# Attention blocks taken in six pairs, with TensorE's row halves and column halves in alternation

## The chip, the cores and the metric

The kernel runs on one core of a Trainium2 chip. The metric is the device time of one execution in microseconds (us); lower is better. The engines are named as the profile names them: PE (TensorE, the matrix multiplier; PEld is its weight load), DVE (VectorE), ACT (ScalarE), POOL (GpSimd) and SP (SyncE, which here only issues DMAs). Each engine works through its own list of instructions in order, and semaphores hold an instruction back until what it reads has been written.

## What is computed

A two-layer decoder trunk on 256 tokens of width 1024: a feed-forward block (SwiGLU), a Mamba-2 mixer, a feed-forward block, the shared keys and values, a feed-forward block, sliding-window attention, a feed-forward block. The change touches the attention alone:

```python
def sliding_window_attention(u, k, v, w_q, q_norm, sinks, rel_bias, w_o):
    q = rmsnorm((u @ w_q).reshape(bsz, t, KV_HEADS, GROUP, HEAD_DIM), q_norm)
    ...
    def block(args):
        s = jnp.einsum('bqkrd,bskd->bkrqs', qk, kk) * scale + bias
        s = jnp.where(valid, s, -jnp.inf)
        m = jnp.maximum(jnp.max(s, axis=-1, keepdims=True), sink)
        p = jnp.exp(s - m)
        denom = jnp.sum(p, axis=-1, keepdims=True) + jnp.exp(sink - m)
        return jnp.einsum('bkrqs,bskd->bqkrd', (p / denom), vk)
    o = lax.map(block, (qb, kb, vb, jnp.arange(nb)))
    return o.reshape(bsz, t, HEADS * HEAD_DIM) @ w_o
```

There are 16 heads of 64, two key/value heads (eight query heads share one), and two tiles of 128 tokens; the first tile sees 128 keys, the second 256.

## The kernel before

All products with weights are made in a split form: a weight tile `raw` is loaded by DMA, ACT casts it to a rounded part `wh` (line 167), DVE subtracts to get the rest `wl` (line 168), and PE adds three products (`wh,vh`, `wl,vh`, `wh,vl`). The products inside attention, queries with keys and weights with values, are plain float32, and each of those matrix products is two passes in the trace.

The attention has these steps, by the names in the code. Below, t is the tile of tokens (0 or 1) and g the key/value head (0 or 1).

- Queries of tile t, head group g: 24 products into a bank `pq` (`q_mm`). `q_norm` then takes ACT (square, line 955), DVE (sum, line 957), POOL (power, line 218, output `rq`) and DVE (multiply, line 960, output `qn`). `q_turn`, called Q, transposes `qn` on PE into `ptq`, and ACT copies it to `qT` (line 971).
- The work on heads is cut into 12 blocks. A block of tile 0 has four heads of 128 keys, a block of tile 1 has two heads of 256 keys. Even blocks use the lower 64 partitions of `qT` and `kT` (row half 0 of PE), odd blocks the upper 64.
- `scores` (Sc): PE writes `ps`; DVE copies the sink into the last column of `sp`, and one custom instruction for each head adds the bias and takes the maximum (`CUSTOM_DVE_ANT_0` in the trace, `ISA` in the lists below); DVE negates it to `nmx`.
- `expo` (E): ACT, one exponential for each head, with the sum in `den`.
- `divide` (D): DVE, reciprocal `rd` and one multiplication for each head.
- `weights_T` (W): PE transposes `sp` into `ptp`; ACT copies it to `pT` (line 985).
- `values` (V): PE multiplies `pT` with the values into `po`; even blocks write PSUM partitions 0 to 63 (column half 0), odd ones 64 to 127. After the last block of a (t, g), ACT casts `po` into `uT` and DVE writes the rest of it (both through `act` and `dve`).

`act` and `dve` chain these steps on ACT and DVE in the order of the calls. With `strict` set, PE's instructions stand exactly in the order of the code. Between the blocks stand fills, one for each call of `F(1)`: three products of the queries of g = 1 (16 fills), and then three products of the output projection `pa` for the first half of the heads (32 fills). The splits of `w_o`, which those need, go to ACT and DVE between the other work, from the time when the buffers of `w_q` come free.

Before, the queries of both tiles of g = 0 are computed with the weight tiles in the outer loop, and the statistics of the norm (`cur.stats`, PE's `pc`) come 42 products into them. Then the loop runs over 12 blocks with these lags: W four blocks behind Sc, V five, E one, D two. `ps` has two banks of its own; `ptp` and `po` share two banks (`ps_tr`). `sp` has five buffers.

Of the kernel before, what the change touches and what calls it, by code (L numbers as in the profile page):

```python
# [18 lines left out]
P = 128  # L19
# [21 lines left out]
def yoco_kernel(ctx: ExitStack, tc: tile.TileContext, a: dict, out: bass.AP):  # L41
# [896 lines left out]
    def attention(ap, cur, kT, vtok, bias, nxt):  # L938
# [52 lines left out]
        def scores(n):  # L991
            t, g, b, nh = blocks[n]
            qT = qTs[t, g]
            L = (t + 1) * P
            i = b % 2
            p0 = (b // 2) * nh
            ps = ps_mm.tile([P, nh, L], F32, tag="mm", name=nm("ps"))
            sp = ap.tile([P, nh, L + 1], F32, tag="sp", name=nm("sp"), bufs=5)
            mx = sb.tile([P, 4], F32, tag="mx", name=nm("mx"), bufs=5)
            nmx = sb.tile([P, 4], F32, tag="nmx", name=nm("nmx"), bufs=5)  # L1000
            den = sb.tile([P, 4], F32, tag="den", name=nm("den"), bufs=5)
            rd = sb.tile([P, 4], F32, tag="rd", name=nm("rd"), bufs=5)
            hs = [(p0 + x) * 2 + i for x in range(nh)]
            for x in range(nh):
                j = p0 + x
                mm(ps[:, x, :], qT[i * DH:(i + 1) * DH, j * P:(j + 1) * P],
                   kT[g][i * DH:(i + 1) * DH, 0:L], True, True)
            dve(nc.vector.tensor_copy, sp[:, :, L], snk[:, g * 8 + hs[0]:g * 8 + hs[-1] + 1:2])
            for x in range(nh):
                hh = g * 8 + hs[x]  # L1010
                dve(nc.vector.tensor_tensor_reduce,
                    out=sp[:, x, 0:L], in0=ps[:, x, :], in1=bias[g][:, hs[x], S - L:S],
                    scale=1.0, scalar=snk[:, hh:hh + 1], op0=ALU.add, op1=ALU.max,
                    accum_out=mx[:, x:x + 1])
            dve(nc.vector.tensor_scalar_mul, nmx[:, 0:nh], mx[:, 0:nh], -1.0)
            sps[n] = sp, nmx, rd, den

        def expo(n):
            sp, nmx, rd, den = sps[n]
            for x in range(blocks[n][3]):  # L1020
                act(nc.scalar.activation, sp[:, x, :], sp[:, x, :], AF.Exp,
                    bias=nmx[:, x:x + 1], accum_out=den[:, x:x + 1])

        def divide(n):
            t, g, b, nh = blocks[n]
            L = (t + 1) * P
            sp, nmx, rd, den = sps[n]
            dve(nc.vector.reciprocal, rd[:, 0:nh], den[:, 0:nh])
            for x in range(nh):
                dve(nc.vector.tensor_scalar_mul, sp[:, x, 0:L], sp[:, x, 0:L], rd[:, x:x + 1])  # L1030
# [13 lines left out]
        def values(n):  # L1044
            t, g, b, nh = blocks[n]
            nk = t + 1
            i = b % 2
# [4 lines left out]
            for kk in range(nk):  # L1052
                mm(po[i * DH:(i + 1) * DH, p0 * P:(p0 + nh) * P],
                   vtok[kk][:, g * DH:(g + 1) * DH], pTs[n][:, kk, :], kk == 0, kk == nk - 1)
            if b == 8 // nh - 1:
# [45 lines left out]
        later(42, cur.stats)  # L1101
        strict[0] = True
        pqs = [q_bank() for t in range(NT)]
        for k in range(KT):
            for t in range(NT):
                q_mm(pqs[t], t, 0, k)
        for t in range(NT):
            q_norm(pqs[t], t, 0)
        F(5)
        Q(0, 0)  # L1110
        F(1)
        fills = (2, 2, 2, 2, 1, 1, 0, 0, 0, 0, 0, 5, 5, 5, 5, 4, 4)
# [126 lines left out]
```

## Time and profile before

| | us |
|---|---|
| median of 3 runs | 1044.66 (1044.32 to 1045.03) |
| the profiled execution's own time | 1044.65 |
| its span, first to last instruction | 1042.9 |
| PE, DVE, ACT, POOL busy in the span | 1031.1, 738.8, 605.6, 56.1 |
| attention on PE, from the first `pq` to the first `pm` behind it | 769.9 to 852.3 of the span |

A row of the time line has the start (us from the span's start), the duration, the engine, the line, the operation, the output and inputs by the program's names, the array tile (`64*128` is 64 rows by 128 columns), the shape and the number of merged instructions; in brackets stands how long the engine idled before it and what ended that. Lines 102 and 989 and 985 are helpers, so the steps are told apart by their tiles.

### The profile page before, as it was taken

The page shows a single profiled execution, that of the slowest core. Times are in us where ns is not written, and L with a number is a line of the kernel's source. Part 1 is how long each engine was busy: PE and PEld are TensorE (multiplying, and loading weights), DVE is VectorE, ACT ScalarE, POOL GpSimd, SP SyncE. Part 2 cuts the span into 40 slices and gives each one's busy share as a digit, 9 for nine tenths or more (in the row PEclk, how much of TensorE's full clock was granted, in tenths as well). Part 3 has the DMA queues.
Part 4 walks back from the last instruction along what each step waited for, and adds up shares of the span by engine and source line. Part 5 has one row for each costly group of instructions (what it writes and reads, how often), then busy time and mean ns, then how long its engine had stood idle before and what let it go on. Part 6 is the DMA issues. An engine that isn't in the chain of part 4 may idle for free.

```text
span 1042.9 us, 17921 instructions
## 1 busy us (share of the span) xinstructions
PE 1031.1 (99%) x7096; PEld 942.7 (90%) x7096; DVE 738.8 (71%) x1260; ACT 605.6 (58%) x1048; POOL 56.1 (5%) x78
## 2 busy tenths in 40 slices
PE   9999999999999999999999999999999999999998
PEld 8999999999999999999998999999986699888887
DVE  6965656789999889656556975665677678565654
ACT  7654545668966656454545754454566665454552
POOL 1200000003210010000000000010002000000000
PEclk9999999999999999999999999999999999999999
DMA  8665556557455364746566556584641336464641
GB/s 283 200 219 196 185 180 209 157 176 247 163 160 184 124 204 162 233 160 213 162 203 194 169 164 201 165 294 163 229 162 41 122 106 214 166 209 158 216 145 41
DMA packets 138981, 187.17 MB, mean 179 GB/s; under 512 B 5005, under 2 KB 120881, under 8 KB 138897
## 3 DMA queue, kind: packets, MB, share of 16 engines
q1 hardware_dynamic: 136560, 179.32, 52.6%
q0 software_dynamic: 2288, 6.69, 2.3%
q8 instruction: 55, 0.90, 0.4%
q14 instruction: 30, 0.24, 0.1%
q10 hardware_dynamic: 48, 0.02, 0.0%
HBM read 184.90 MB, written 1.11 MB: 178 GB/s over the span
## 4 chain that ended last, share of the span: by engine, by line
PE 68%; issue 21%; DVE 5%; DMA 2%; POOL 2%; ACT 1%; SPq 0%; POOLq 0%; DVEq 0%; ACTq 0%
PE pm L104 36%; PE acc L104 17%; PE pa L104 5%; PE pp L104 3%; DVE wl L168 2%; PE pq L102 2%; PE pa L102 1%; PE ps L102 1%; PE po L102 1%; DVE sp L989 1%; DMA xin<-in_x_dram 1%; DMA raw<-in_ssm_w_out_dram 1%; PE pkv L104 1%; PE py L104 1%; DMA raw<-in_ssm_w_in_dram 1%
## 5 line engine op out<-in xcount | busy, mean ns | idle before, releaser
L168 DVE TENSOR_TENSOR wl<-raw,wh 128x1024 fp32r<-128x1024 f32 (+1 forms) x372 | 411.7, 1129 | 82.2 <-ACT wh L167 80.5
L167 ACT CAST wh<-raw 128x1024 fp32r<-128x1024 f32 (+1 forms) x372 | 347.1, 970 | 108.7 <-PE acc L104 44.7
L104 PE MATMUL pm<-uT,wh 128*128 128x512 f32 x1152 | 403.1, 392 | 0.8 <-DVE tp L326 0.8
L104 PE MATMUL pm<-uT,wl 128*128 128x256 f32 x1152 | 321.5, 280 | 0.0
L104 PEld LDWEIGHTS pm<-uT,wh 128*128 128x128 f32 x1152 | 216.1, 188 | 46.5 <-ACT wdth L532 1.0
L104 PEld LDWEIGHTS pm<-uT,wl 128*128 128x128 f32 x1152 | 216.6, 188 | 0.9
L104 PE MATMUL acc<-ghl,wh 128*128 128x256 f32 x1056 | 191.5, 282 | 1.6 <-DVE ghl L344 1.4
L335 ACT COPY lo<-pm 128x256 f32<-128x256 f32 x144 | 53.2, 369 | 205.9 <-PE pm L104 205.9
L104 PEld LDWEIGHTS acc<-ghl,wh 128*128 128x128 f32 x1056 | 162.2, 188 | 4.9 <-DVE ghl L344 1.9
L336 DVE TENSOR_TENSOR tp<-pm,lo 128x256 f32<-128x256 f32 x144 | 60.9, 423 | 135.4 <-ACT lo L335 135.3
L104 PE MATMUL acc<-ghl,wl 128*128 128x256 f32 x528 | 148.2, 282 | 0.0
L104 PE MATMUL pp<-uT,wh 128*128 128x256 f32 x576 | 104.9, 283 | 0.1
L104 PEld LDWEIGHTS acc<-ghl,wl 128*128 128x128 f32 x528 | 99.4, 188 | 0.0
L104 PEld LDWEIGHTS pp<-uT,wh 128*128 128x128 f32 x576 | 88.6, 189 | 0.5 <-DVE uT L300 0.3
L104 PE MATMUL pp<-uT,wl 128*128 128x256 f32 x288 | 80.5, 281 | 0.0
L104 PE MATMUL pm<-vh,wh 128*128 128x256 f32 x256 | 73.2, 286 | 0.0
L104 PE MATMUL pm<-vh,wl 128*128 128x256 f32 x256 | 72.5, 283 | 0.0
L104 PE MATMUL pm<-vl,wh 128*128 128x256 f32 x256 | 72.4, 283 | 0.0
L104 PE MATMUL acc<-wh,ghl 128*128 128x512 f32 x176 | 58.3, 395 | 0.0
L343 ACT CAST ghl<-g 128x256 fp32r<-128x256 f32 x88 | 35.4, 403 | 32.9 <-DVE g L340 32.5
L104 PEld LDWEIGHTS pp<-uT,wl 128*128 128x128 f32 x288 | 54.1, 188 | 0.2 <-issue 0.2
L344 DVE TENSOR_TENSOR ghl<-g,ghl 128x256 fp32r<-128x256 f32 x88 | 37.0, 422 | 17.7 <-ACT ghl L343 17.7
(234 smaller groups left out, 1268.1 us busy)
## 6 DMA issues: line engine op xcount, KB each, us to landing
raw<-in_ffn_w_dram SPq DMA_DIRECT2D x168, 512.0 KB, 4.9
raw<-in_ffn_w_dram SPq DMA_DIRECT2D x44, 1024.0 KB, 5.3
raw<-in_ssm_w_in_dram SPq DMA_DIRECT2D x16, 1024.0 KB, 5.4
raw<-in_ssm_w_out_dram SPq DMA_DIRECT2D x8, 1024.0 KB, 5.2
raw<-in_ssm_w_in_dram SPq DMA_DIRECT2D x8, 512.0 KB, 5.1
pr<-pdram POOLq DMA_DIRECT2D x8, 512.0 KB, 4.4
raw<-in_w_q_dram SPq DMA_DIRECT2D x4, 1024.0 KB, 4.9
raw<-in_w_o_dram SPq DMA_DIRECT2D x4, 1024.0 KB, 4.8
```

What stands on the lines that cost most here:

```text
L102: r = op(*args, **kw)
L104: r = op(*args, **kw)
L167: return (nc.scalar.copy(wh, rs).ins, nc.vector.tensor_sub(wl, rs, wh.bitcast(F32)).ins)
L168: nc.vector.tensor_sub(wl, rs, wh.bitcast(F32)).ins)
L335: nc.scalar.copy(lo, pw[:, 256:512])
L336: nc.vector.tensor_add(o, pw[:, 0:256], lo)
L343: nc.scalar.copy(gh, g)
L344: nc.vector.tensor_sub(gl, g, gh.bitcast(F32))
L989: chain[1] = op(*args, **kw).ins
```

## The change

The loop runs over six pairs of blocks instead of 12 blocks. In a pair, Sc alternates its products between the two row halves and two `ps` banks; V alternates between the two column halves of `po`. The copy of the sink goes from DVE to POOL (`nc.gpsimd`), `sp` and its companions get six buffers. The queries of tile 0, g = 0 are computed in full before those of tile 1, and the statistics come 20 products in. The order within one round m is W of the first block of pair m-2, Sc of pair m, E of pair m, W of the second block of pair m-2, V of pair m-3, D of pair m-1, then the fills.

```diff
-        def scores(n):
+        def scores(m):
...
-            for x in range(nh):
-                j = p0 + x
-                mm(ps[:, x, :], qT[i * DH:(i + 1) * DH, j * P:(j + 1) * P],
-                   kT[g][i * DH:(i + 1) * DH, 0:L], True, True)
-            dve(nc.vector.tensor_copy, sp[:, :, L], snk[:, g * 8 + hs[0]:g * 8 + hs[-1] + 1:2])
...
             for x in range(nh):
+                for i in range(2):
+                    mm(pss[i][:, x, :], qT[i * DH:(i + 1) * DH, (p0 + x) * P:(p0 + x + 1) * P],
+                       kT[g][i * DH:(i + 1) * DH, 0:L], True, True)
+            for i in range(2):
+                sp, mx, nmx, den = sps[2 * m + i]
+                h0 = g * 8 + p0 * 2 + i
+                nc.gpsimd.tensor_copy(sp[:, :, L], snk[:, h0:h0 + 2 * nh - 1:2])
...
-        def values(n):
+        def values(m):
...
             for kk in range(nk):
-                mm(po[i * DH:(i + 1) * DH, p0 * P:(p0 + nh) * P],
-                   vtok[kk][:, g * DH:(g + 1) * DH], pTs[n][:, kk, :], kk == 0, kk == nk - 1)
-            if b == 8 // nh - 1:
+                for i in range(2):
+                    mm(po[i * DH:(i + 1) * DH, p0 * P:(p0 + nh) * P],
+                       vtok[kk][:, g * DH:(g + 1) * DH], pTs[2 * m + i][:, kk, :], kk == 0, kk == nk - 1)
+            if p0 + nh == 4:
...
-        later(42, cur.stats)
+        later(20, cur.stats)
         strict[0] = True
-        pqs = [q_bank() for t in range(NT)]
-        for k in range(KT):
-            for t in range(NT):
-                q_mm(pqs[t], t, 0, k)
         for t in range(NT):
-            q_norm(pqs[t], t, 0)
-        F(5)
+            pq = q_bank()
+            for k in range(KT):
+                q_mm(pq, t, 0, k)
+            q_norm(pq, t, 0)
         Q(0, 0)
-        F(1)
-        fills = (2, 2, 2, 2, 1, 1, 0, 0, 0, 0, 0, 5, 5, 5, 5, 4, 4)
-        qs = {0: (1, 0), 3: (0, 1), 7: (1, 1)}
-        lw, lv, ld = 4, 5, 2
-        last = len(blocks)
-        for n in range(last + lv):
-            for fn, m in ((W, n - lw), (V, n - lv), (Sc, n), (E, n - 1), (D, n - ld)):
-                if 0 <= m < last:
-                    fn(m)
-            F(fills[n])
-            if n in qs:
-                Q(*qs[n])
+        fills = (5, 5, 6, 0, 0, 10, 8, 8, 6)
+        qs = {0: (1, 0), 2: (0, 1), 3: (1, 1)}
+        last = len(blocks) // 2
+        for m in range(last + 3):
+            if 0 <= m - 2 < last:
+                W(2 * (m - 2))
+            if m < last:
+                Sc(m)
+                E(m)
+            if 0 <= m - 2 < last:
+                W(2 * (m - 2) + 1)
+            if 0 <= m - 3:
+                V(m - 3)
+            if 0 <= m - 1 < last:
+                D(m - 1)
+            F(fills[m])
+            if m in qs:
+                Q(*qs[m])
```

How this moves the instructions is best seen where head group 1 begins. On PE, before, a block at that place (`ps_1517` are the scores of the first block of g = 1):

```order
L102 MATMUL ptp_1515_9347<-anti_104,sp_1481_9224 128x128 x4
L102 MATMUL po_1504_9316<-pT_1503_9314,v0_7730 64x512
L102 MATMUL ps_1517_9357<-kT1_7501,qT_1493_9280 128x128 x4
L102 MATMUL ptp_1523_9378<-anti_104,sp_1487_9251 128x128 x4
L102 MATMUL po_1525_9385<-pT_1516_9352,v0_7730 64x256
L102 MATMUL po_1525_9385<-pT_1516_9352,v1_7855 64x256
L102 MATMUL ps_1526_9388<-kT1_7501,qT_1493_9280 128x128 x4
```

On PE, in the changed kernel, from the end of pair 3's scores (`ps_1514` and `ps_1519`, the first pair of g = 1) to those of pair 4 (`ps_1533`):

```order
L102 MATMUL ps_1519_9357<-kT1_7501,qT_1511_9343 128x128
L102 MATMUL ptp_1524_9390<-anti_104,sp_1479_9206 128x128 x4
L102 MATMUL po_1526_9397<-pT_1491_9268,v0_7730 64x512
L102 MATMUL po_1526_9397<-pT_1503_9301,v0_7730 64x512
L102 MATMUL ptq_1529_9410<-anti_104,qn_1506_9329 128x128 x4
L102 MATMUL ptp_1531_9417<-anti_104,sp_1493_9271 128x128 x4
L102 MATMUL ps_1533_9424<-kT1_7501,qT_1530_9415 128x256
```

Between the scores of two pairs now stand W, V, Q and the next W; no fill stands there. On ACT, before, around the cast of the first `po` into `uT`:

```order
L985 ACTIVATE sp_1497_9290,den_1500_9293<-sp_1497_9290,nmx_1499_9292 128x257 x2
L955 ACTIVATE qn_1511_9338<-pq_1479_9216 128x512
L985 COPY pT_1516_9352<-ptp_1515_9347 128x512
L985 CAST uT_110<-po_1504_9316 128x4x128
L167 CAST wh_1578_9560<-raw_1577_9558 128x512
L985 ACTIVATE sp_1506_9319,den_1509_9322<-sp_1506_9319,nmx_1508_9321 128x257 x2
```

On ACT, in the changed kernel, around the same cast:

```order
L971 COPY qT_1530_9415<-ptq_1529_9410 128x512
L985 ACTIVATE sp_1515_9353,den_1518_9356<-sp_1515_9353,nmx_1517_9355 128x129 x4
L167 CAST wh_1580_9572<-raw_1579_9570 128x512
L985 ACTIVATE sp_1520_9358,den_1523_9361<-sp_1520_9358,nmx_1522_9360 128x129 x4
L985 COPY pT_1525_9395<-ptp_1524_9390 128x512
L985 CAST uT_110<-po_1526_9397 128x4x128
```

Before, two exponentials stood ahead of the cast; now it has the eight of pair 3 ahead of it. On DVE, in the changed kernel, behind the last maximum of pair 3 (`nmx_1522`):

```order
L989 TENSOR_SCALAR nmx_1522_9360<-mx_1521_9359 128x4
L168 TENSOR_TENSOR wl_1576_9559<-raw_1574_9556,wh_1575_9558 128x512
L168 TENSOR_TENSOR wl_1578_9561<-raw_1574_9556,wh_1577_9560 128x512 x2
L168 TENSOR_TENSOR wl_1581_9573<-raw_1579_9570,wh_1580_9572 128x512 x2
L989 TENSOR_TENSOR uT_110<-po_1526_9397,uT_110 128x4x128
L989 RECIPROCAL rd_1527_9402<-den_1496_9274 128x2
L168 TENSOR_TENSOR wl_1583_9575<-raw_1579_9570,wh_1582_9574 128x512
L989 TENSOR_SCALAR sp_1493_9271<-sp_1493_9271,rd_1527_9402 128x256 x2
```

The division of pair 2 (`rd_1527`, `sp_1493`), which the transposes `ptp_1531` on PE read, now stands behind the `uT` subtraction, which reads ACT's cast.

More of the change, by code (lines that the diff above doesn't have):

```diff
@@ L989, in dve @@
                 chain[1] = op(*args, **kw).ins
-        def scores(n):
-            t, g, b, nh = blocks[n]
+        def scores(m):
+            t, g, b, nh = blocks[2 * m]
             qT = qTs[t, g]
             L = (t + 1) * P
-            i = b % 2
             p0 = (b // 2) * nh
[L997 to L1003, printed above, removed]
-            for x in range(nh):
-                j = p0 + x
-                mm(ps[:, x, :], qT[i * DH:(i + 1) * DH, j * P:(j + 1) * P],
-                   kT[g][i * DH:(i + 1) * DH, 0:L], True, True)
-            dve(nc.vector.tensor_copy, sp[:, :, L], snk[:, g * 8 + hs[0]:g * 8 + hs[-1] + 1:2])
-            for x in range(nh):
[L1010 to L1030, printed above, removed]
+            pss = []
@@ new lines, in scores @@
+            for i in range(2):
+                pss.append(ps_mm.tile([P, nh, L], F32, tag="mm", name=nm("ps")))
+                sps[2 * m + i] = [ap.tile([P, nh, L + 1], F32, tag="sp", name=nm("sp"), bufs=6)]
+                for w in ("mx", "nmx", "den"):
+                    sps[2 * m + i].append(sb.tile([P, 4], F32, tag=w, name=nm(w), bufs=6))
+            for x in range(nh):
+                for i in range(2):
+                    mm(pss[i][:, x, :], qT[i * DH:(i + 1) * DH, (p0 + x) * P:(p0 + x + 1) * P],
+                       kT[g][i * DH:(i + 1) * DH, 0:L], True, True)
@@ new lines, in scores @@
+            for i in range(2):
+                sp, mx, nmx, den = sps[2 * m + i]
+                h0 = g * 8 + p0 * 2 + i
+                nc.gpsimd.tensor_copy(sp[:, :, L], snk[:, h0:h0 + 2 * nh - 1:2])
+                for x in range(nh):
+                    dve(nc.vector.tensor_tensor_reduce,
+                        out=sp[:, x, 0:L], in0=pss[i][:, x, :], in1=bias[g][:, (p0 + x) * 2 + i, S - L:S],
+                        scale=1.0, scalar=snk[:, h0 + 2 * x:h0 + 2 * x + 1], op0=ALU.add, op1=ALU.max,
+                        accum_out=mx[:, x:x + 1])
+                dve(nc.vector.tensor_scalar_mul, nmx[:, 0:nh], mx[:, 0:nh], -1.0)
@@ new lines, in expo, with divide @@
+        def expo(m):
+            for n in (2 * m, 2 * m + 1):
+                sp, mx, nmx, den = sps[n]
+                for x in range(blocks[n][3]):
+                    act(nc.scalar.activation, sp[:, x, :], sp[:, x, :], AF.Exp,
+                        bias=nmx[:, x:x + 1], accum_out=den[:, x:x + 1])
+        def divide(m):
+            for n in (2 * m, 2 * m + 1):
+                t, g, b, nh = blocks[n]
+                L = (t + 1) * P
+                sp, mx, nmx, den = sps[n]
+                rd = sb.tile([P, 4], F32, tag="rd", name=nm("rd"), bufs=4)
+                dve(nc.vector.reciprocal, rd[:, 0:nh], den[:, 0:nh])
+                for x in range(nh):
+                    dve(nc.vector.tensor_scalar_mul, sp[:, x, 0:L], sp[:, x, 0:L], rd[:, x:x + 1])
@@ L1042, in weights_T @@
             act(nc.scalar.copy, pTs[n], pt)
-        def values(n):
-            t, g, b, nh = blocks[n]
+        def values(m):
+            t, g, b, nh = blocks[2 * m]
             nk = t + 1
-            i = b % 2
             p0 = (b // 2) * nh
@@ L1052, in values @@
             for kk in range(nk):
-                mm(po[i * DH:(i + 1) * DH, p0 * P:(p0 + nh) * P],
-                   vtok[kk][:, g * DH:(g + 1) * DH], pTs[n][:, kk, :], kk == 0, kk == nk - 1)
-            if b == 8 // nh - 1:
+                for i in range(2):
+                    mm(po[i * DH:(i + 1) * DH, p0 * P:(p0 + nh) * P],
+                       vtok[kk][:, g * DH:(g + 1) * DH], pTs[2 * m + i][:, kk, :], kk == 0, kk == nk - 1)
+            if p0 + nh == 4:
                 ov = po.rearrange("p (k q) -> p k q", k=4)
```

## The prediction

> **What bounds the kernel now.** I read the page first, then the windows of the attention, then its time line on each engine.
>
> ```profile
> span 1042.9 us, 17921 instructions
> ...
> PE 1031.1 (99%) x7096; PEld 942.7 (90%) x7096; DVE 738.8 (71%) x1260; ACT 605.6 (58%) x1048; POOL 56.1 (5%) x78
> ...
> PE 68%; issue 21%; DVE 5%; DMA 2%; POOL 2%; ACT 1%; SPq 0%; POOLq 0%; DVEq 0%; ACTq 0%
> ```
>
> PE is busy for 99% of the span and carries the chain that ended last, so any time saved or idled on PE counts in full. The windows say how near the others are in the attention (columns: stretch, its length, then busy time of PE, PEld, DVE, ACT, POOL):
>
> ```profile
> 800.00:820.00 20.00, 19.28 (x91) 11.64 (x92) 19.32 (x85) 18.47 (x56) 1.64 (x1) 1.00 0.49 157
> 820.00:842.00 22.00, 22.00 (x145) 17.10 (x144) 7.80 (x28) 7.71 (x18) 0.00 (x0) 1.00 0.16 50
> ```
>
> From 800 to 820 DVE (19.3 of 20) and ACT (18.5) are as full as PE. The softmax there has no slack: a faster PE finds its inputs not yet made.
>
> **What the pairs save on PE.** The time line of PE:
>
> ```profile
> 784.50 0.39 PE L102 MATMUL pq<-wh,vl 128*128 128x512 f32 x1
> 785.56 0.63 PE L102 MATMUL ptq<-anti,qn 128*128 128x128 f32 x4 [0.67 <-DVE qn L960]
> ...
> 786.87 1.16 PE L102 MATMUL ps<-kT,qT 64*128 64x128 f32 x8
> 787.95 0.50 PE L102 MATMUL pq<-wh,vh 128*128 128x512 f32 x1
> ...
> 800.65 0.60 PE L102 MATMUL ptp<-anti,sp 128*128 128x128 f32 x4
> 801.18 1.07 PE L102 MATMUL po<-pT,v 128*64 128x512 f32 x2
> 802.18 1.13 PE L102 MATMUL ps<-kT,qT 64*128 64x256 f32 x4
> 803.24 0.50 PE L102 MATMUL pq<-wh,vh 128*128 128x512 f32 x1
> ...
> 803.81 0.39 PE L102 MATMUL pq<-wh,vl 128*128 128x512 f32 x1
> ...
> 811.88 1.13 PE L102 MATMUL ps<-kT,qT 64*128 64x256 f32 x4 [0.34 <-ACT qT L971]
> ...
> 819.72 1.07 PE L102 MATMUL po<-pT,v 128*64 128x512 f32 x2 [0.27 <-DVE uT L989]
> ```
>
> From start to start a block takes 0.53 for W, 1.00 for V and 1.06 to 1.08 for Sc. If both halves of the array run at once, a pair needs one block's time for Sc and for V: 6 x 1.07 + 6 x 1.00 = **12.4 us** less PE work. PE's own waits in the stage were 0.67 + 0.34 + 0.27 = 1.28 us.
>
> Do halves run at once? For column halves the trace of before has a row, in the Mamba mixer, where `py` alternates 64-column halves:
>
> ```profile
> 264.52 2.22 PE L104 MATMUL py<-em,xdt 128*64 128x256 f32 x24
> ```
>
> These 24 passes are half 256 and half 128 columns wide. A `ps` pass of 256 takes some (1.06 - 0.2)/4 = 0.215 us and one of 128 some (1.08 - 0.2)/8 = 0.11 (0.2 being the change of shape), so one after the other they would need 12 x 0.215 + 12 x 0.11 = 3.9 us. They took 2.2: the halves overlap, and V's 6.0 us is taken in full. For row halves no row exists; Sc's 6.4 us lies between nothing and 6.4, and I take 6.4, as `py` is the nearest row. [...]
>
> **What the new order costs.** PE's list is strict, so each product that needs a result of ACT or DVE holds all behind it. These are the durations (first two groups of the stage, then single rows):
>
> ```profile
> L167 ACT CAST wh<-raw 128x512 fp32r<-128x512 f32 x16 | 9.2, 619 | 0.0
> L168 DVE TENSOR_TENSOR wl<-raw,wh 128x512 fp32r<-128x512 f32 x16 | 10.9, 680 | 0.0
> ```
>
> ```profile
> 775.65 0.42 DVE L267 TENSOR_TENSOR sq<-sq 128x256 f32<-128x256 f32 x1
> ...
> 786.23 0.59 ACT L971 COPY qT<-ptq 128x512 f32<-128x512 f32 x1 [4.12 <-PE ptq L102]
> ...
> 788.06 0.35 DVE L989 CUSTOM_DVE_ANT_0 sp<-ps,bias,snk 128x128 f32<-128x128 f32 x1 [1.04 <-PE ps L102]
> ...
> 788.33 0.35 DVE L989 CUSTOM_DVE_ANT_0 sp<-ps,bias,snk 128x128 f32<-128x128 f32 x1
> ...
> 789.26 0.17 DVE L989 TENSOR_SCALAR nmx<-mx 128x4 f32<-128x4 f32 x1
> ...
> 802.69 0.62 DVE L989 TENSOR_SCALAR sp<-sp,rd 128x256 f32<-128x256 f32 x2
> ...
> 803.35 0.48 DVE L989 CUSTOM_DVE_ANT_0 sp<-ps,bias,snk 128x256 f32<-128x256 f32 x1
> ...
> 803.76 0.48 DVE L989 CUSTOM_DVE_ANT_0 sp<-ps,bias,snk 128x256 f32<-128x256 f32 x1
> ...
> 804.79 0.58 ACT L985 COPY pT<-ptp 128x512 f32<-128x512 f32 x1
> 805.68 0.59 ACT L985 CAST uT<-po 128x512 fp32r<-128x512 f32 x1 [0.31 <-PE po L102]
> 806.03 1.64 POOL L218 TENSOR_TENSOR rq<-me,mhalf 128x8 f32<-128x8 f32 x1 [12.97 <-DVE me L216]
> 806.32 0.68 DVE L989 TENSOR_TENSOR uT<-po,uT 128x512 fp32r<-128x512 f32 x1
> ...
> 808.07 0.68 DVE L960 TENSOR_TENSOR qn<-pq,rq 128x512 f32<-128x512 f32 x1
> ...
> 809.70 0.41 ACT L985 ACTIVATE sp<-sp,nmx 128x129 f32<-128x129 f32 x1
> ...
> 810.10 0.40 ACT L985 ACTIVATE sp<-sp,nmx 128x129 f32<-128x129 f32 x1
> ...
> 815.78 0.53 ACT L985 ACTIVATE sp<-sp,nmx 128x257 f32<-128x257 f32 x1
> ...
> 816.28 0.52 ACT L985 ACTIVATE sp<-sp,nmx 128x257 f32<-128x257 f32 x1
> ```
>
> By starts: a maximum 0.27 (128 keys) or 0.41 (256), an exponential 0.39 or 0.50, a division of two heads 0.62, a cast 0.58 (9.2/16), a subtraction 0.68 (10.9/16). A query norm, from the end of the last `pq` (803.81 + 0.39) to the end of `qn` (808.07 + 0.68), 4.55. A turn, from the first `ptq` to the first `ps` (785.56 to 786.87), 1.31, of which PE works 0.44.
>
> Now the stalls, in PE's order:
>
> 1. The statistics (`pc`) stand 21 products (4.8 us) into the queries, at 774.7 on the old clock; DVE's last sum for them ends at 776.07. Wait **1.35**.
> 2. Q(0,0) stands directly ahead of Sc(0); before, a fill lay between. 1.31 - 0.44 = **0.85**.
> 3. Sc(1) needs Q(1,0), whose copy to `qT` stands on ACT behind seven of the eight exponentials of pair 0. Those wait for Sc(0)'s maxima, and the `qn` multiplication of the tile-1 queries is ahead of these on DVE. From the end of the tile-1 `pq`: 4.55 + 4 x 0.27 + 0.2 + 7 x 0.39 + 0.59 = 9.2. PE has Q, the stall above, Sc(0), five fills (15 x 0.23) and Q: 0.4 + 0.85 + 1.08 + 3.45 + 0.44 = 6.2. Wait **3.0**.
> 4. Sc(3) after Q(0,1), with one W between: 0.85 - 0.44 = 0.4; with `pT` and a query square ahead of the copy on ACT up to 1.4. I take **1.0**.
> 5. Q(1,1) waits for its norm, 4.55 behind the last `pq`; PE's work until then (Q, W, stall 4, Sc, W, V) is 0.44 + 0.44 + 1.0 + 1.08 + 0.53 + 1.0 = 4.5. Bare nothing, with queued work ahead up to 1.0: **0.5**.
> 6. The large one. W of pair 2 needs its division, which DVE has behind the `uT` subtraction, which waits for ACT's cast, behind all of E(3); and the maxima of pair 3 wait behind that same `qn`. From the end of `qn`: four maxima 1.1, one subtraction 0.68, `nmx` 0.17, four exponentials 1.56, a cast 0.58, four exponentials 1.56, `pT` 0.48, the `uT` cast 0.59, the subtraction 0.60, one more 0.68, the division 0.62: 8.6. PE has Q(1,1), 0.5. Wait **8.1**; with none of the weight work in between 6.2.
> 7. W of pair 3's first block needs the bank that `pT` of pair 2 frees, behind E(4): 2 x 0.41 + 0.2 + 4 x 0.50 + 0.58 = 3.6 from Sc(4); PE has W and V, 1.5. Wait **2.1**.
> 8. The first `pa` needs `uT` of V(2), behind E(5): 0.8 + 0.2 + 2.0 + 0.48 + 0.59 + 0.69 = 4.8; PE has 1.5. Wait **3.3**.
>
> The sum is 1.35 + 0.85 + 3.0 + 1.0 + 0.5 + 8.1 + 2.1 + 3.3 = **20.2 us**, or 17.2 with the small ends of 4, 5 and 6. Less the 1.28 of before it is 18.9 more waiting against 12.4 saved: **+6.5 us**.
>
> Costed at nothing: the sink copies leave DVE (12 x 0.07 of its time between starts, hidden before under PE) and go to POOL. No POOL copy is in the trace; between DVE's 0.16 and POOL's 1.64 for 8 columns I take the lower. On POOL, `rq` of the last two norms stands behind such a copy, and these wait for W on PE; for the last one that W ends about when `rq`'s own input comes, so stall 6 covers it. At 1.64 each it would add some 1.5 to stalls 5 and 6 together. The DMAs of `w_o` wait for buffers as before and land in 4.8 us; the feed-forward behind the attention starts later as a whole, since its weight buffers come free only with the output projection.
>
> **The clock.** PE has never idled 2 us in this stage, and now would for 8. What that does is seen at both ends of the run:
>
> ```profile
> 5.54 1.06 PE L1153 MATMUL px<-ident,xin 128*128 128x128 f32 x4
> ...
> 12.09 0.60 PE L1153 MATMUL px<-ident,xin 128*128 128x128 f32 x4
> ```
>
> ```profile
> 1038.00:1040.00 2.00, 1.18 (x6) 0.61 (x4) 1.29 (x2) 0.00 (x0) 0.00 (x0) 1.00 0.62 234
> 1040.00:1042.90 2.90, 0.00 (x0) 0.00 (x0) 0.00 (x0) 0.00 (x0) 0.00 (x0) 0.75 0.31 112
> ```
>
> Four transposes took 1.06 us at the start and 0.60 later; after PE's last product (by 1039.2) the granted clock fell, to a mean of 0.75 in the last 2.9 us, that is to half at about 1041.4. So 2 to 3 us of idleness halve the clock, and stalls 6 and perhaps 8 bring it. Then W and Sc behind stall 6 (0.53 + 1.07) cost as much again, and either the same work behind stall 7 or the fills behind stall 8 (10 x 0.35) do: 1.6 to 5 us. I take **3**. [...]
>
> Forecast: the profiled execution's own time, 1044.65, which is also the median to 0.01, + 6.5 + 3 = **1054.2 us**.
>
> **The rivals.**
> - The waits come but the clock stays up: 1044.65 + 6.5 = 1051. For it: the idle spell is broken by a turn and part of a W. Chance 0.22.
> - The row halves don't overlap. Then 6.4 of the saving go, but Sc(1), Sc(3) and Sc(4) stand between stalls and only move what waits: +1.5 to +6.4, so 1056 to 1060. For it: no row shows them. Chance 0.15.
> - Faster: the softmax runs ahead of PE, since pairs reach DVE and ACT half a pair earlier. It decides if the stalls stay below 12.4 + 1.3 = 13.7, which needs stall 6 at 1.6 or less, as if E(3) did not stand ahead of the cast. With no stall 6 at all it would be 1044.65 - 12.4 + (12.1 - 1.3) = 1043. Against it: the lists of ACT and DVE, and the 1.56 + 1.56 us of exponentials in them. Chance 0.07.
> - The change does what it says and nets little: stalls at their bare ends, no clock loss, 17.2 - 1.3 - 12.4 = +3.5, so 1048; with 2 us less of stall 6 it would be no change. Chance 0.08, half of it for no change.
>
> **How the numbers follow.** The forecast itself (1052 to 1057) has 0.48. The range runs from the bare ends without a clock loss (1048, less 0.5) to no overlap of rows with it (1060): 1047.5 to 1060. A measurement of this kernel can tell 0.2% (2 us) from no change: slower 0.48 + 0.22 + 0.15 + 0.04 = 0.89, same 0.04, faster 0.07.
>
> **What would show it.** Right: PE idle of 7 us or more in one piece shortly after the last `ptq`, released by DVE's division of `sp` or ACT's `pT`; a wait of some 3 us ahead of the first `pa`, released by DVE `uT`; a clock below 1.00 in those windows; V pairs in 1.0 us, Sc pairs in 1.1. Wrong: `ps` pairs in 2.1 us (rows don't overlap); PE busy above 95% from the first `ps` to the last `po` (the softmax kept pace); a longer feed-forward behind the attention (weights late).

## The result, and the profile after

The changed kernel takes **1054.61 us** (median of 4 runs, 1052.24 to 1055.50) beside 1044.79 for the kernel before in the same comparison: a ratio of 1.0095, 95% interval 1.0083 to 1.0107. The forecast was 1054.2. The profiled execution took 1055.5 us.

The page of the changed kernel: span, busy times, the row of the granted clock, and the engines of the chain that ended last.

```profile
span 1053.8 us, 17938 instructions
...
PE 1023.2 (97%) x7096; PEld 939.5 (89%) x7096; DVE 739.4 (70%) x1248; ACT 605.5 (57%) x1048; POOL 59.5 (6%) x90
...
PEclk9999999999999999999999999999999799999999
...
PE 67%; issue 18%; DVE 8%; DMA 3%; ACT 2%; POOL 1%; SPq 0%; ACTq 0%; DVEq 0%; POOLq 0%
```

PE is busy for 7.9 us less and the span is 10.9 us longer, so PE now waits, and DVE's share of the chain rises from 5% to 8%. Nearly all of it lies in one place. These are the windows from the first query product to the first product of the feed-forward behind the attention, first of the kernel before, then of the changed one (columns: stretch, length, busy time of PE, PEld, DVE, ACT, POOL, granted clock, DMA share, GB/s):

```profile
769.93:852.27 82.34, 80.94 (x462) 61.68 (x461) 57.24 (x197) 50.83 (x131) 7.23 (x5) 1.00 0.29 97
```

```profile
770.88:863.11 92.23, 72.69 (x462) 58.11 (x461) 57.52 (x185) 50.73 (x131) 9.12 (x11) 0.91 0.25 87
```

The stage is 9.9 us longer, as much as the medians differ (9.8). Of the span's 10.9 the other 1.0 us lies ahead of the stage, which starts at 770.88 instead of 769.93, in code that the change leaves alone; the feed-forward behind it takes 190.7 us beside 190.6, so the weights are not late there. The number of PE's instructions is the same, 462; PE is busy for 8.3 us less although its clock was lower; the work of DVE and ACT has not changed by half a microsecond. The time line of PE in this stage shows where it waits (start, duration, what it does; in brackets the idle time before it and what ended it):

```profile
776.99 0.61 PE L102 MATMUL pc<-mean,sq 128*128 128x1 f32 x4 [1.16 <-DVE sq L267]
...
785.00 1.16 PE L102 MATMUL ps<-kT,qT 64*128 64x128 f32 x16 [0.73 <-ACT qT L971]
...
792.60 1.14 PE L102 MATMUL ps<-kT,qT 64*128 64x256 f32 x8 [2.37 <-ACT qT L971]
...
804.63 0.63 PE L102 MATMUL ptp<-anti,sp 128*128 128x128 f32 x4 [0.58 <-DVE sp L989]
806.26 1.16 PE L102 MATMUL ps<-kT,qT 64*128 64x128 f32 x16 [1.00 <-ACT qT L971]
...
807.94 1.08 PE L102 MATMUL po<-pT,v 128*64 128x512 f32 x4
810.21 0.66 PE L102 MATMUL ptq<-anti,qn 128*128 128x128 f32 x4 [1.19 <-DVE qn L960]
818.47 1.09 PE L102 MATMUL ptp<-anti,sp 128*128 128x128 f32 x4 [7.61 <-DVE sp L989]
819.49 2.08 PE L102 MATMUL ps<-kT,qT 64*128 64x256 f32 x8
...
825.41 0.74 PE L102 MATMUL ptp<-anti,sp 128*128 128x128 f32 x4 [1.81 <-ACT pT L985]
...
832.48 0.44 PE L102 MATMUL pa<-uT,wh 128*128 128x256 f32 x1 [2.22 <-ACT uT L985]
```

With three of 0.29 behind these, the waits come to 19.5 us, against 1.28 before. A pair of score blocks (x16, x8) takes 1.16 and 1.14 us, as long as one block took before (1.16, 1.13); where it takes 2.08, the clock is at half. The granted clock (third column from the end) in stretches of 3.41 and 3.42 us:

```profile
808.78:812.19 3.41, 0.89 (x6) 0.42 (x4) 2.73 (x14) 2.31 (x5) 0.78 (x2) 1.00 0.00 0
812.19:815.60 3.41, 0.00 (x0) 0.00 (x0) 3.41 (x12) 3.41 (x17) 0.00 (x0) 0.50 0.70 220
...
819.02:822.43 3.41, 3.41 (x15) 2.02 (x13) 1.59 (x7) 0.59 (x1) 0.19 (x1) 0.50 0.86 265
822.43:825.84 3.41, 1.60 (x13) 0.90 (x12) 3.11 (x18) 2.56 (x9) 0.19 (x1) 1.00 0.46 158
825.84:829.26 3.42, 3.42 (x17) 2.03 (x16) 1.04 (x6) 0.59 (x1) 0.00 (x0) 0.50 0.00 0
829.26:832.67 3.41, 1.19 (x9) 0.58 (x9) 1.20 (x7) 3.04 (x10) 0.00 (x0) 1.00 0.00 0
832.67:836.08 3.41, 3.12 (x14) 2.88 (x14) 1.86 (x7) 0.00 (x0) 0.00 (x0) 0.50 0.02 5
```

The clock is at half in 812.19 to 822.43, 825.84 to 829.26 and 832.67 to 836.08, each time behind a stretch in which PE was busy for less than half (0.89, 1.60 and 1.19 of 3.41 us). From 812.19 to 815.60 PE does nothing at all, while ACT and DVE are busy for every moment of it: ACT with the exponentials of pair 3 and a cast of `w_o`, DVE with its maxima and with splits of `w_o`, all ahead of what PE waits for. The two lists reach the step that the division stands behind, the `uT` subtraction, at the same moment: the fifth split of a run on DVE ends at 816.67, ACT's cast into `uT` at 816.68.

```profile
816.10 0.58 ACT L985 CAST uT<-po 128x512 fp32r<-128x512 f32 x1
...
813.58 3.09 DVE L168 TENSOR_TENSOR wl<-raw,wh 128x512 fp32r<-128x512 f32 x5
816.71 0.69 DVE L989 TENSOR_TENSOR uT<-po,uT 128x512 fp32r<-128x512 f32 x1
```

So the long wait is held twice, by the exponentials on ACT and by the maxima and splits on DVE; by these rows an earlier cast alone would not have shortened it.

### The profile page after: what moved, and what is told of

It reads as the page before. It is cut to its first block, busy times and chain, and to the rows that moved or that the text cites. A ratio compares the mean times of both kernels' runs of the same rounds, so it can differ in the third digit from the quotient of the medians.

```text
span 1053.8 us, 17938 instructions
## 1 busy us (share of the span) xinstructions
PE 1023.2 (97%) x7096; PEld 939.5 (89%) x7096; DVE 739.4 (70%) x1248; ACT 605.5 (57%) x1048; POOL 59.5 (6%) x90
## 4 chain that ended last, share of the span: by engine, by line
PE 67%; issue 18%; DVE 8%; DMA 3%; ACT 2%; POOL 1%; SPq 0%; ACTq 0%; DVEq 0%; POOLq 0%
PE pm L104 35%; PE acc L104 16%; PE pp L104 5%; PE pa L104 5%; DVE wl L168 3%; PE pa L102 1%; DMA raw<-in_ssm_w_in_dram 1%; DVE sp L989 1%; ACT sp L985 1%; DMA xin<-in_x_dram 1%; DVE vl L254 1%; DMA raw<-in_ssm_w_out_dram 1%; PE pq L102 1%; POOL rq L218 1%; PE py L104 1%
```

## The experiments

The theory: the pairs save what was forecast; the loss is waits that come from the new order of the work on ACT and DVE, and half clock behind them. The rivals: the sink copies on POOL, halves that overlap only in part, or a softmax that cannot go faster in any order. All ratios below are against the kernel before, with 95% intervals.

### The sink copies back on DVE

```diff
-                nc.gpsimd.tensor_copy(sp[:, :, L], snk[:, h0:h0 + 2 * nh - 1:2])
+                dve(nc.vector.tensor_copy, sp[:, :, L], snk[:, h0:h0 + 2 * nh - 1:2])
```

> The changed kernel with one part undone: the twelve copies of the sinks go back from POOL to DVE. In the trace of the changed kernel such a copy takes 0.19 us on POOL and `rq` 1.64 to 2.01 behind it. Theory (the copies cost nothing on either engine, as the prediction had it): 1054.6, within 0.2%, and the wait ahead of the transposes of pair 2's weights stays at 7.4 to 8.0 us. Rival (POOL's copies hold the query norms up, the bound of 1.5 us in the prediction): 1053.1, with the wait ahead of the last query transposes falling from 1.36 to under 0.5.

Measured: 1053.73 us, 1.0089 (1.0073 to 1.0105), not to be told from the changed kernel's 1.0095. Within it the waits moved, which neither side expected. On DVE the eight maxima of pair 3 now came ahead of the query norm's multiplication, since only `act` and `dve` chain their order and the norm does not. The time line of PE in this run:

```profile
809.69 1.09 PE L102 MATMUL ptq<-anti,qn 128*128 128x128 f32 x4 [3.22 <-DVE nmx L989]
815.31 1.08 PE L102 MATMUL ptp<-anti,sp 128*128 128x128 f32 x4 [4.53 <-DVE sp L989]
```

The wait ahead of the query's transposes grew by 2.0 us and the long one behind it fell by 3.1. The copies cost nothing that these runs can tell, though the shift on DVE came with their return and the two effects were not taken apart.

### Halves not alternating

```diff
-            for x in range(nh):
-                for i in range(2):
+            for i in range(2):
+                for x in range(nh):
                     mm(pss[i][:, x, :], qT[i * DH:(i + 1) * DH, (p0 + x) * P:(p0 + x + 1) * P],
...
-                for i in range(2):
+            for i in range(2):
+                for kk in range(nk):
                     mm(po[i * DH:(i + 1) * DH, p0 * P:(p0 + nh) * P],
```

> The changed kernel with the two halves no longer alternating: all score products of the first block of a pair, then all of the second; for the values of two key tiles both products of the first half, then both of the second. Theory A (each half of the array runs its own products whatever their order in PE's list, as `py` of the trace of before suggests): 1054.6 within 0.2%, score pairs still in 1.1 to 1.2 us, value pairs in 1.0 to 1.1. Theory B (halves overlap only where neighbours in the list differ): score pairs take 2.1 us and the value pairs of two key tiles 1.5 to 2; four of the six score pairs stand on the way to the next wait, so 1054.6 + 4 to 8 = 1058 to 1062.

Measured: 1054.32 us, 1.0095 (1.0082 to 1.0108): no difference in time, as theory A had it, and a value pair of two key tiles still takes 1.09 us. The scores of a 128-key and of a 256-key pair on PE's time line:

```profile
783.77 1.71 PE L102 MATMUL ps<-kT,qT 64*128 64x128 f32 x16 [0.73 <-ACT qT L971]
791.76 1.14 PE L102 MATMUL ps<-kT,qT 64*128 64x256 f32 x8 [2.22 <-ACT qT L971]
```

Theory A holds in full only for the second: four passes for each half, in 1.14 us as before. With eight passes for each half the pair takes 1.71 instead of 1.16, more than alternating and less than the 2.1 of one after the other (2 x 1.07). So halves that stand apart in the list still overlapped in these two rows, in full at four passes each and in part at eight. The 0.55 us, which two of the six pairs can lose, does not show in the time: the waits and the stretches of half clock fell differently in this run (from 781 to 848 a mean clock of 0.85 beside 0.87).

### The statistics later

```diff
-        later(20, cur.stats)
+        later(27, cur.stats)
...
-            q_norm(pq, t, 0)
-        Q(0, 0)
+            if k == 0:
+                q_norm(pqs[0], 0, 0)
+        q_norm(pqs[1], 1, 0)
+        Q(0, 0)
```

> The changed kernel with the statistics 27 instead of 20 products into the queries, behind the first step of the second tile; the first tile's norm is called behind them. Theory (step 1 of the prediction: PE stands still for 1.32 us at `pc`, and everything behind is late by that): no wait ahead of `pc`, the second tile's queries end 1.3 us sooner, and the maxima of pair 0, which stand behind their norm, too: 1053.3. Rival (the wait comes back one step later: the first query transposes then wait for the first norm, whose statistics come no sooner): a new wait of 0.7 to 1.3 us ahead of the first `ptq`, but the total still falls by what the second norm gains, 0.6 to 1.3; or, if the first norm is on the way, 0 to 0.6.

Measured: 1055.32 us, 1.0108 (1.0093 to 1.0122): nothing gained. Both expectations missed the place. The time line of PE:

```profile
776.74 0.50 PE L102 MATMUL pq<-wl,vh 128*128 128x512 f32 x1 [1.52 <-DVE wl L168]
```

The wait at `pc` is gone, and one of 1.52 us stands at the last step of the first tile's queries, for the split of the last part of `w_q` on DVE. With the tiles one after the other PE needs that part after 22 products; with the tiles alternating, as before, after 43. The `pc` wait had hidden this one.

### PE kept busy in the three long waits

```diff
+        def idle_work(n):
+            pw = ps_acc.tile([P, P], F32, tag="acc", name=nm("pw"))
+            for i in range(n):
+                mm(pw, ident, ident, True, True)
...
+            if m == 5:
+                idle_work(9)
             F(fills[m])
             if m in qs:
                 Q(*qs[m])
+            if m in (3, 4):
+                idle_work((30, 8)[m - 3])
```

> The changed kernel with products of the identity with itself, whose results nobody reads, in the three long waits: 30 behind the last query transposes, 8 behind the values of pair 1, 9 ahead of the first `pa`; at some 0.22 us each they fill 6.5 of 7.8, 1.7 of 2.0 and 2.0 of 2.4 us and should end before what PE waits for is there. They compute nothing of the output. Clock theory (the waits halve PE's granted clock for 3.4 us each, and the work in these windows takes twice its time): the clock stays at 1.00, the transposes and scores behind the long wait take 0.53 + 1.1 instead of 1.1 + 2.1, the same behind the second wait, and fills 0.35 instead of 0.7: 1.6 + 1.6 + 1.7 = 4.9 us less, 1049.7; with part of it taken up by the next wait 1051 to 1052. Rival (the lower clock costs nothing, as the softmax sets the pace there anyway): 1054.6 within 0.2%.

Measured: 1051.61 us, 1.0073 (1.0061 to 1.0085), 0.22% or 2.3 us below the changed kernel. PE's time line at the long wait:

```profile
811.54 0.66 PE L102 MATMUL ptq<-anti,qn 128*128 128x128 f32 x4 [1.19 <-DVE qn L960]
812.03 6.86 PE L102 MATMUL pw<-ident 128*128 128x128 f32 x60
819.80 0.63 PE L102 MATMUL ptp<-anti,sp 128*128 128x128 f32 x4 [0.91 <-DVE sp L989]
820.36 1.13 PE L102 MATMUL ps<-kT,qT 64*128 64x256 f32 x8
```

From `ptq` to `ptp` it is 8.26 us (819.80 less 811.54), as in the changed kernel (818.47 less 810.21): the added products do not touch the wait. What follows does change. From that `ptp` to the first product behind the stage, in the changed kernel and in this one:

```profile
818.47:863.11 44.64, 39.74 (x276) 32.93 (x277) 22.06 (x65) 18.57 (x41) 0.37 (x2) 0.88 0.25 85
```

```profile
819.80:860.78 40.98, 39.26 (x310) 33.72 (x311) 22.04 (x65) 18.58 (x41) 0.53 (x2) 1.00 0.28 92
```

With the clock at 1.00 this stretch is 3.66 us shorter, though PE runs 34 more passes in it. The price of half clock in this stretch of the profiled execution is therefore about 3.7 us, so the softmax does not cover it. The two ratios alone would hardly have decided that, as their intervals just touch. Ahead of this stretch the clock did fall once in the run with added products (last section), and its stage as a whole is 3.1 us shorter, not 3.7.

### Only the values paired, or both, in the old order

The first edit pairs the values of the kernel before and leaves all else; the second pairs the scores as well, in the same way, at the even block's turn.

```diff
         def values(n):
...
-            if b == 0:
+            if b % 2 == 0:
+                return
+            if b == 1:
                 pos[t, g] = ps_tr.tile([P, 512], F32, tag="tr", name=nm("po"))
...
-                mm(po[i * DH:(i + 1) * DH, p0 * P:(p0 + nh) * P],
-                   vtok[kk][:, g * DH:(g + 1) * DH], pTs[n][:, kk, :], kk == 0, kk == nk - 1)
+                for i in range(2):
+                    mm(po[i * DH:(i + 1) * DH, p0 * P:(p0 + nh) * P],
+                       vtok[kk][:, g * DH:(g + 1) * DH], pTs[n - 1 + i][:, kk, :], kk == 0, kk == nk - 1)
```

```diff
-            for x in range(nh):
-                j = p0 + x
-                mm(ps[:, x, :], qT[i * DH:(i + 1) * DH, j * P:(j + 1) * P],
-                   kT[g][i * DH:(i + 1) * DH, 0:L], True, True)
+            if i == 0:
+                for ii in range(2):
+                    pss[n + ii] = ps_mm.tile([P, nh, L], F32, tag="mm", name=nm("ps"))
+                for x in range(nh):
+                    for ii in range(2):
+                        mm(pss[n + ii][:, x, :], qT[ii * DH:(ii + 1) * DH, (p0 + x) * P:(p0 + x + 1) * P],
+                           kT[g][ii * DH:(ii + 1) * DH, 0:L], True, True)
+            ps = pss[n]
```

> The kernel before with one part of the change alone: the values of two blocks of a pair are multiplied together, alternating between the column halves, when the second block's turn comes; loop, queries, scores, softmax order as before. Theory (pairing saves what the prediction put it at, 6 x 1.0 us, and the loss comes from the new order alone): 1044.3 - 6.0 = 1038.3, or 1040 with 2 us of it taken up by a wait for the softmax where DVE and ACT were as busy as PE. Rival (the softmax sets the pace of the attention, so any faster PE only waits): 1044.3 within 0.2%, with 6 us more idle time on PE.

> The kernel before with both pairings and the old order of the softmax: scores of two blocks together at the first block's turn, values at the second's, everything else (queries, maxima, exponentials, divisions, transposes, one block at a time) as before. Theory (PE's saving is 12.4 us, but the softmax of the second half has its own pace in this order): between 1044.3 - 12.4 = 1032 and the 1038 to 1040 of the values alone; what PE saves more than those is likely met by waits ahead of the transposes of the weights, 1036 to 1040. Rival (pairing itself costs the time, the bursts of two blocks hold ACT and DVE up): slower than with the values alone by the loss of the change, 1050 or more.

Measured: with the values alone 1042.47 us, 0.9981 (0.9972 to 0.9989); with both 1041.13, 0.9968 (0.9956 to 0.9980). Pairing makes the kernel faster in the old order, so it is not what costs the time. But it brings 1.7 and 3.1 us, not 6.0 and 12.4. The stage with both paired, and its largest wait on PE:

```profile
769.54:848.73 79.19, 69.35 (x462) 55.30 (x461) 57.01 (x197) 50.85 (x131) 7.67 (x5) 0.98 0.31 101
```

```profile
815.52 1.07 PE L102 MATMUL ptp<-anti,sp 128*128 128x128 f32 x4 [2.03 <-DVE sp L989]
```

PE is busy for 11.6 us less than the 80.94 of the kernel before, and 8.4 of it is given back (idle time 9.84 instead of 1.40 us) as waits of 0.3 to 2.0 us, spread over the stage: the old order was made for a slower PE. Both expectations were too good, by 1 to 5 us here and by 2.5 to 4 with the values alone. There the idle time is 3.2 us, 1.8 more than before, and the clock takes a part that the expectations left out: the profiled run has a mean granted clock of 0.91 from 800 to 820, where the kernel before has 1.00, and the two of its twelve runs with a recorded mean clock of 1.000 took 1040.2 and 1040.8 us, the seven with 0.993 to 0.995 took 1042.2 to 1044.0.

### Two orders inside a round

The first edit puts a round's transposes, copies and values ahead of the next scores and exponentials, the second only moves the divisions ahead of the values.

```diff
             if 0 <= m - 2 < last:
                 W(2 * (m - 2))
+                W(2 * (m - 2) + 1)
+            if 0 <= m - 3:
+                V(m - 3)
             if m < last:
                 Sc(m)
                 E(m)
-            if 0 <= m - 2 < last:
-                W(2 * (m - 2) + 1)
-            if 0 <= m - 3:
-                V(m - 3)
```

> The changed kernel with only the order inside a round changed: both transposes of the weights, the values and with them the copies to `pT` and the `uT` cast stand ahead of the next pair's scores and exponentials, not between and behind them. Theory (step 6: the long wait is W of pair 2 behind its division, behind `uT`, behind all of the exponentials of pair 3): these exponentials, 8 x 0.39 = 3.1 us, leave the way to the division and to the bank, so the long wait falls from 7.8 to some 4.5 and, as less of the clock is lost, 1054.6 - 3 to 6 = 1049 to 1051.5. Rival (the maxima behind the late query norm set it): the wait stays above 7 us and the time within 0.3% of 1054.6.

```diff
-            if 0 <= m - 3:
-                V(m - 3)
             if 0 <= m - 1 < last:
                 D(m - 1)
+            if 0 <= m - 3:
+                V(m - 3)
```

> The changed kernel with one link of the long wait's chain taken out: the divisions of the pair before stand ahead of the values of three pairs before, so that on DVE they no longer wait behind the `uT` subtraction. Theory (what comes next is right behind: the bank of the transposes is freed by `pT` on ACT, which stands behind all exponentials of pair 3 as well, and only the `uT` cast, its subtraction and a queued split, 0.5 + 0.6 + 0.6, leave the way): the long wait falls from 7.8 to some 6.5, 1053 to 1054. Rival (the subtraction was the whole of it): the wait falls below 5, 1051 or less.

Measured: 1051.98 us, 1.0064 (1.0051 to 1.0076) for the first, 1053.81, 1.0087 (1.0074 to 1.0101) for the second. In the first, PE and DVE around the old place of the long wait:

```profile
812.68 1.09 PE L102 MATMUL ptq<-anti,qn 128*128 128x128 f32 x4 [4.38 <-DVE rd L989]
...
821.66 1.09 PE L102 MATMUL ptp<-anti,sp 128*128 128x128 f32 x4 [2.69 <-DVE sp L989]
```

```profile
808.12 0.68 DVE L989 TENSOR_TENSOR uT<-po,uT 128x512 fp32r<-128x512 f32 x1
...
809.80 0.23 DVE L216 TENSOR_SCALAR me<-ss,eps 128x8 f32<-128x8 f32 x1
```

The wait of 7.6 us is broken up: 4.4 now stand ahead of the last query, whose norm (`me`) waits on DVE behind the `uT` subtraction and four maxima, and 2.7 ahead of the weights of pair 2. The time fell by 3.2 us (0.0031), the small end of what was expected. In the second, the long wait falls to 5.4 us and has another releaser, as theory had it:

```profile
815.97 1.11 PE L102 MATMUL ptp<-anti,sp 128*128 128x128 f32 x4 [5.38 <-ACT pT L985]
```

With the division out of the way, the bank of the transposes is next: `pT` on ACT, behind the exponentials of pair 3. The wait shrank by 2.2 us, more than the 1.3 expected, but the time by no more than the intervals allow for.

### A new order, and a new order without pairs

Each step is a letter (S scores, M maxima, E exponentials, D division, W transposes, C copy, V values, U and T the two parts of `uT`, N and X norm and multiplication of a query, Q its turn, O and o the splits of `w_o`, G and F steps of queries and output), and one list sets the order on PE, ACT and DVE at once. The list comes from a search over such orders with the durations of the traces; its first two lines:

```diff
+        order = """
+            G G G G F G G N0.0 G G X0.0 Q0.0 F F S0 N1.0 M1 X1.0 M0 E1 F F D1 F
+            F Q1.0 F N0.1 S1 F M3 M2 F E0 F F O0 O2 O6 S2 E2 X0.1 D0 O1 Q0.1 M4 F M5
...
+        for s in order.split():
+            with tc.high_priority():
+                fns[s[0]](*(int(c) for c in s[1:].split(".") if c))
```

> The changed kernel's pairs with every step of the stage placed by hand, one list for all engines: the parts of a pair (maxima, exponentials, divisions, transposes, copies, norm and multiplication of a query, splits of `w_o`) are steps of their own, each put where the durations of the traces say that its input is there and that it is not in the way of one needed sooner; the products of the second tile's and second group's queries lie between them. The same arithmetic. Theory (waits are a matter of order alone; DVE and ACT have enough room in the stage as a whole): PE's waits in the attention fall from 21.5 us to 2 to 5, so the stage takes 82.3 - 12.4 + 0 to 3 = 70 to 73 us and the kernel 1032 to 1035. Rival (DVE and ACT cannot keep the pace of the pairs in any order): waits of 8 us or more, 1040 or above.

Measured: **1033.19 us**, 0.9891 (0.9878 to 0.9903). The stage, and PE's time in scores and values there, first for the kernel before and then for this one:

```profile
781.00:848.00 67.00, 13.65 (x64) 9.20 (x64) 11.73 (x32) 1.00 0.26 82
...
781.00:848.00 67.00, 12.91 (x40) 4.49 (x40) 2.75 (x4) 2.35 (x4) 1.00 0.26 82
```

```profile
771.01:841.28 70.27, 67.37 (x462) 54.63 (x461) 58.10 (x184) 50.37 (x131) 8.99 (x11) 1.00 0.34 112
...
781.00:848.00 67.00, 6.86 (x64) 4.70 (x64) 11.72 (x32) 1.00 0.33 106
...
781.00:848.00 67.00, 6.49 (x40) 2.34 (x40) 2.67 (x4) 2.35 (x4) 1.00 0.33 106
```

The scores fall from 13.65 to 6.86 us, the values from 12.91 to 6.49: 13.2 us less by busy time, and with no half clock in the stage and 2.9 us of waits most of it arrives: the stage is 12.1 us shorter, the kernel 11.0. DVE and ACT do nearly the same work as in every other version (58.1 and 50.4 of 70.3 us): over the whole stage they were not too slow, they were asked in the wrong order. The largest wait left:

```profile
777.73 0.50 PE L102 MATMUL pq<-wl,vh 128*128 128x512 f32 x1 [1.52 <-DVE wl L168]
```

That is the one found with the later statistics. The next edit puts three steps of the other tile ahead of it.

```diff
         for k in range(KT):
+            if k == KT - 1:
+                for i in range(3):
+                    next(q0)
             q_mm(pqs[0, 0], 0, 0, k)
```

> The new order with three steps of the second tile's queries moved ahead of the last step of the first tile's. In the new order PE still waits 1.69 us there for the split of the last part of `w_q` on DVE (`pq<-wl`). Theory (the products of the other tile cover it, as they did in the kernel before, whose two tiles alternate): the wait is gone, 1033.2 - 1.0 to 1.7 = 1031.5 to 1032.2. Rival (the first tile's norm comes later and the wait returns ahead of the first query transposes): 1033.2 within 0.1%.

Measured: **1031.12 us**, 0.9881 (0.9865 to 0.9898). The wait is gone, and the stage takes 68.88 us instead of 70.27. The median is 2.1 us lower, slightly more than the 1.0 to 1.7 of the theory; the ratio's interval alone would not tell it from 0.9891.

The last one keeps the blocks of a pair apart: S and V do the first block, new letters s and v the second, and another list sets the order.

```diff
             for x in range(nh):
-                for i in range(2):
-                    mm(pss[i][:, x, :], qT[i * DH:(i + 1) * DH, (p0 + x) * P:(p0 + x + 1) * P],
-                       kT[g][i * DH:(i + 1) * DH, 0:L], True, True)
+                mm(pss[0][:, x, :], qT[0:DH, (p0 + x) * P:(p0 + x + 1) * P], kT[g][0:DH, 0:L], True, True)
...
+            rest["s", m] = second
...
+            part(0)
+            rest["v", m] = lambda: part(1)
```

> The stage placed by hand as in the new order, but with the two blocks of a pair kept apart: between the scores of its first and second block, and between their values, stands a product that uses the whole array, so that no two halves can run at once. Tells what of the new order's 11 us is the pairing and what the order. Theory (the pairing is worth 12.4 us of PE's work, and the kernel before, with 2.1 us of waits in the stage, had little to gain from its order): 1033.2 + 9 to 12 = 1042 to 1045, PE's waits 1 to 5 us. Rival (the order alone brings it): below 1038.

Measured: 1041.94 us, 0.9980 (0.9972 to 0.9989). This order brings 0.2%; the pairing, with its own order, 0.9% on top of it, some 9 us. The kernels do not differ in the pairing alone, as each has its own list, and the pairing was not fully taken away: in three places blocks of different halves from two pairs stand one directly behind the other. By their times, beside some 2.1 us for two blocks one after the other, two of these overlapped in part (1.87, 1.61) and the third in full (1.14):

```profile
791.93 1.87 PE L102 MATMUL ps<-kT,qT 64*128 64x128 f32 x12
...
795.77 1.61 PE L102 MATMUL ps<-kT,qT 64*128 64x256 f32 x8
...
813.42 1.14 PE L102 MATMUL ps<-kT,qT 64*128 64x256 f32 x8
```

PE is busy with scores for 11.47 us and with values for 12.63, against 13.65 and 12.91 before the change and 6.86 and 6.49 with pairs: some 2.5 of the 13.2 us remained, so that the 9 us stand beside a difference of 10.8. Here, nearly as in the new order (1.52), 1.48 us of waiting for `w_q` remain.

## Why the prediction was right

- **What the pairs save** (12.4 us): right. A pair takes the time of one block for scores (1.16, 1.14) and for values (1.08). The new order, which has no half clock, shows 13.2 by busy time; the forecast counted from start to start, which gives some 0.07 us less for each block. The open question, whether row halves overlap, is settled for halves that alternate: 16 passes of 128 take 1.16 us, as 8 of one half did before, and 8 of 256 take 1.14 beside 1.13 for 4. The scores' busy time falls by 6.8 us.
- **Stalls 1 and 2** (1.35, 0.85): measured 1.16 and 0.73. The cause given for the first was one of two. The experiment showed that the split of `w_q`'s last part, which the prediction did not look at, ends just as late, so that removing the wait for the statistics brings nothing.
- **Stalls 3 to 5** (3.0, 1.0, 0.5): measured 2.37, then 0.58 and 1.00, then 1.19. The W ahead of the scores of pair 3 took a wait of its own for its division; the sum is 5.1 against 4.5.
- **Stall 6** (8.1, W of pair 2): 7.61, in one piece, released by the division as written. From the end of `qn` (810.15) to the wait's end (818.47) it is 8.3 us, 8.6 in the sum. With only the division moved the wait falls to 5.4 and `pT`, behind the exponentials of pair 3, becomes the releaser: that much is theirs, as shown. For the other 2.2 us DVE's own list held the division as long as ACT's did, which the prediction overlooked: it counted one split between `qn` and the `uT` subtraction, where seven stood, and the last of them ended with ACT's cast. With the copies and values ahead of both exponentials and maxima the wait breaks up, but that order moved both lists, so it does not part them.
- **Stalls 7 and 8** (2.1, 3.3): 1.81 and 2.22 + 0.29. The second was put too high, and the first `pa` waits for ACT's `uT` first and only for 0.29 us, one product later, for DVE's. The sum of all is 19.5 against 20.2; less the 1.28 of before 18.3 against 18.9.
- **The clock** (3, from 1.6 to 5): 3.7 in the profiled execution, 2.3 between the medians. It came with stall 6, as forecast, but also with stalls 7 and 8, each below 3 us; the prediction had left those open. Its reading that 2 to 3 us of idle time halve the clock was too simple: half clock came with stall 7 (1.81) and not with stall 3 (2.37), as the last section shows. The start of the run of before, which it read beside the end, has a granted clock of 1.00 (3.00 to 9.00), so the slow transposes there are no sign of half clock in that trace. How long half clock lasts, on which the range rests, no row of before shows; in the changed kernel it lasted 10.24 us with stall 6, in which PE worked for 3.96, and 3.42 and 3.41 us with stalls 7 and 8.
- **The sum**: 18.3 of waits - 12.4 + 3.7 = 9.6 us, of 9.9 in the stage. The errors, waits 0.6 less and clock 0.7 more, nearly cancel. The 3.7 is a net figure, as with the clock up the waits behind it differ a little, so the sum is good to some tenths only. That the median came within 0.4 us of the forecast is in part luck: the four runs spread over 3.3 us.
- **The rivals**: the clock did fall, so 1051 is out; row halves overlap, so 1056 to 1060 is out; stall 6 came nearly whole, so neither the faster case nor that of the bare ends. That a faster outcome was possible with these pairs is shown by the new order; that the softmax has no slack, where the prediction started, holds for the lists of this kernel between 800 and 820 us and not for the stage as a whole, in which DVE was busy for 57.2 and ACT for 50.8 of 82.3 us.
- **Sink copies at nothing**: on POOL they take 0.18 to 0.46 us in the profile after, with a median of 0.19, near the lower bound of 0.16, and putting them back changed nothing that could be measured in the time.

## What to carry to other kernels

When a stage in which several engines are nearly full gets faster on one of them, the order of the work on the others can decide who gains, as it did here: write out, for each result that the faster engine needs, all that stands ahead of it on its producer, and move the steps apart (maxima, exponentials, division, copy) rather than whole blocks. The same pairs cost 0.95% in one order and save 1.19% in another, with nearly the same work on DVE and ACT. And a wait that is removed has often covered another: before counting it as saved, look for what is next late at the same place.

## What the hardware showed beside this

- **A half's products did not all wait for those of the other half ahead of them.** The list with all products of one row half first took 1.14 us for a pair with four passes in each half, beside 1.13 for one block alone, and 1.71 us instead of 1.16 with eight. So products of the second half ran beside products of the first that stand ahead of them, in full in the one case and in part in the other, and the statement at the top that each engine works through its list in order does not describe PE there. What sets the difference was not tried.
- **The length of a wait did not tell whether the clock halved.** In the changed kernel the granted clock was 0.50 for 10.24 us from 812.19, for 3.42 us from 825.84 and for 3.41 us from 832.67, with the waits of 7.61, 1.81 and 2.22 us. The wait of 2.37 us ahead of the second pair's scores left it at 1.00; in the run with added products the wait at the same place was followed by 0.50. First the run with added products (the stretch with the wait, then the next), then the changed kernel:

```profile
791.31:794.72 3.41, 1.39 (x9) 0.98 (x10) 0.22 (x1) 2.37 (x11) 0.00 (x0) 1.00 0.00 0
794.72:798.13 3.41, 3.41 (x9) 2.65 (x8) 3.27 (x19) 2.09 (x8) 0.00 (x0) 0.50 0.01 2
```

```profile
788.29:791.71 3.42, 1.94 (x11) 1.41 (x9) 2.10 (x16) 2.44 (x13) 0.00 (x0) 1.00 0.00 0
791.71:795.12 3.41, 2.52 (x14) 1.92 (x15) 1.32 (x6) 1.40 (x6) 0.00 (x0) 1.00 0.00 0
```

No limit comes out of these runs. With the later statistics PE waited 2.38 us at this place, and the scores behind it took 1.13 us, as at full clock. With the values alone paired it waited 0.99 us ahead of four transposes (815.59), and these took 1.08 us instead of 0.63, in the stretch with a mean clock of 0.91. What decides was not tried. Runs of the changed kernel spread over 3.3 us (1052.24 to 1055.50) at mean clocks of 0.990 to 0.994, those of the new order, whose largest wait in the stage is 1.52 us, over 1.5 (1032.35 to 1033.88) at 0.998 to 1.000. That the clock makes the difference fits, but was not tried.
